# Cross-entropy with label smoothing: other transfer widths, and a second row that follows into the first row's buffers

## The chip, the cores and the metric

The kernel runs on one core of one Trainium2 chip. The metric is device time in microseconds (us). Most executions agree within 0.3%. Kernels are compared only within the same rounds.

## The reference

For 256 rows of 32000 float32 logits, with one label each and smoothing 0.1:

```
log_probs = logits - max(logits); log_probs -= log(sum(exp(log_probs)))
targets   = 0.1/32000 everywhere, + 0.9 at the label
out       = -sum(targets * log_probs)        # one number per row
```

What is costly is one sum of exponentials (ScalarE) and one plain sum (VectorE) over 32.77 MB, which must be read once.

## The kernel before

Each of 128 partitions holds two rows, one after the other in memory. A row arrives in tiles of some thousand columns over all partitions. Per tile, VectorE adds the two halves of the tile and accumulates, and ScalarE takes exponentials and accumulates; what they write besides the sums is scratch that nobody reads (`jd`, `ja`, `jt`). The second row's tiles get narrower, so that little is left to do after the last byte.

```python
WIDTHS = (
    (8000, 8000, 8000, 8000),
    (8000, 6272, 4736, 3648, 2688, 2048, 1536, 1216, 1024, 832),
)
RING_MIN = 4736
TURN_MAX = 3648
...
    ring = ctx.enter_context(tc.tile_pool(name="ring", bufs=3))
    tail = ctx.enter_context(tc.tile_pool(name="tail", bufs=1))
    junk = ctx.enter_context(tc.tile_pool(name="junk", bufs=1))
    turn = ctx.enter_context(tc.tile_pool(name="turn", bufs=3))
...
    def load(w: int, col: int, name: str):
        if w >= RING_MIN:
            xt = ring.tile([P, max(WIDTHS[0])], FP32, name="xt", tag="xt")
        else:
            xt = tail.tile([P, w], FP32, name=name, tag=name)
        ...   # the very first tile in two halves, on the SyncE and ScalarE queues
            nc.sync.dma_start(out=xt[:, :w], in_=x[:, col : col + w])
...
    def sum_exps(xt, w: int, out: bass.AP) -> None:
        if w > TURN_MAX:
            ja = junk.tile([P, max(WIDTHS[0])], BF16, name="ja", tag="ja")   # one buffer
        else:
            ja = turn.tile([P, TURN_MAX], BF16, name="jt", tag="jt")         # three in turn
        nc.scalar.activation(out=ja[:, :w], in_=xt[:, :w], func=AF.Exp, accum_out=out)
```

After the last tile: the logarithm (Ln) of the last row's sum on ScalarE, two transposes on TensorE, two small operations on VectorE, and one transfer of 1 KB out.

The softmax here doesn't subtract the row's maximum and nothing guards it: scores larger than these inputs give would overflow.

## Time and profile before

| | before |
|---|---|
| time, median of 6 runs | 84.85 us (84.72 to 84.95) |
| span in the profile | 83.2 us |
| last tile | 832 columns, exponential from 79.24 us, Ln from 80.20 us |
| busy: ScalarE, VectorE | 58.8 us, 37.1 us |

The span runs from the first to the last instruction; the time is some 1.8 us longer. Read the profile from its end. ScalarE and VectorE wait for the same transfer for each tile. VectorE is the faster one, so it is nearly always waiting when a tile lands: its starts are a clock for the stream. The lines are in the prediction.

### The profile page before, as it was taken

To read this page: it belongs to the slowest core of one execution; us is meant where nothing else is said; L and a number is where in the kernel's file an instruction comes from. 1 tells how busy PE (TensorE), PEld (TensorE's weight loads), DVE (VectorE), ACT (ScalarE), POOL (GpSimd) and SP (SyncE) were. 2 spreads that over 40 slices of the span, in tenths; PEclk is the share of its full clock that TensorE was granted. 3 is DMA by queue.
4 is the path that set the end of the run, shared out by engine and by line. 5 is a ranking of instruction groups with operands and counts; after the bars stand their busy time and mean duration, and the time that the engine had idled before them with its cause. 6 is when DMAs were issued, how large, how long until landed. Compare 5 with 4: busy or idle time off the path is not lost.

```text
span 83.2 us, 230 instructions
## 1 busy us (share of the span) xinstructions
PE 7.0 (8%) x23; PEld 5.0 (6%) x23; DVE 37.1 (45%) x35; ACT 58.8 (71%) x31; POOL 5.7 (7%) x19
## 2 busy tenths in 40 slices
PE   0000000000000000000000010000000000899020
PEld 0000000000000000000000000000000000787000
DVE  0000005950495009910397017922944736754860
ACT  5000005997499809994399908997999999999960
POOL 3201640031000000000000040000000000000000
PEclk9999999999999999999999999999999999999995
DMA  5999999997999899989998998998999999999600
GB/s 131 416 416 408 454 423 462 477 447 323 477 493 431 369 431 493 446 369 416 493 462 354 416 439 386 495 447 370 428 420 414 442 407 415 412 414 412 256 0 0
DMA packets 2258, 32.77 MB, mean 394 GB/s; under 512 B 337, under 2 KB 338, under 8 KB 850
## 3 DMA queue, kind: packets, MB, share of 16 engines
q1 hardware_dynamic: 2018, 30.72, 87.4%
q10 hardware_dynamic: 144, 2.05, 5.8%
q0 software_dynamic: 96, 0.00, 0.1%
HBM read 32.77 MB, written 0.00 MB: 394 GB/s over the span
## 4 chain that ended last, share of the span: by engine, by line
DMA 64%; ACT 32%; issue 1%; SPq 0%; PE 0%; DVE 0%; ACTq 0%
DMA xt<-in_logits_dram 40%; DMA xl<-in_logits_dram 23%; ACT ja L188 17%; ACT jt L188 15%; SPq L167 0%; PE lse_t L193 0%; DVE res L284 0%; ACT lse L279 0%; ACTq L188 0%
## 5 line engine op out<-in xcount | busy, mean ns | idle before, releaser
L188 ACT ACTIVATE ja<-xt 128x8000 bf16<-128x8000 f32 (+2 forms) x7 | 43.9, 6276 | 20.1 <-DMA xt<-in_logits_dram 20.0
L173 DVE SCALAR_TENSOR_TENSOR jd<-xt 128x4000 f32<-128x4000 f32 (+2 forms) x7 | 27.7, 3954 | 33.6 <-DMA xt<-in_logits_dram 33.6
L188 ACT ACTIVATE jt<-xl 128x3648 bf16<-128x3648 f32 (+6 forms) x7 | 12.2, 1748 | 0.1
L173 DVE SCALAR_TENSOR_TENSOR jd<-xl 128x1824 f32<-128x1824 f32 (+6 forms) x7 | 7.9, 1125 | 5.2 <-DMA xl<-in_logits_dram 5.0
L270 PE MATMUL warm<-xl,ident 128*128 128x256 f32 x20 | 6.1, 471 | 21.4 <-DMA xl<-in_logits_dram 21.4
L270 PEld LDWEIGHTS warm<-xl,ident 128*128 128x128 f32 x20 | 4.8, 246 | 22.5 <-DMA xl<-in_logits_dram 21.7
L193 PE MATMUL loss_t<-ident,loss 128*1 128x128 f32 x1 | 0.4, 372 | 49.2 <-POOL loss L224 49.2
L193 PEld LDWEIGHTS loss_t<-ident,loss 128*1 128x1 f32 x1 | 0.1, 79 | 49.2 <-POOL loss L224 49.2
L226 DVE COPY res<-loss_t 1x128 f32<-1x128 f32 x1 | 0.3, 278 | 4.5 <-PE loss_t L193 4.5
L211 POOL TENSOR_TENSOR half<-sums 128x4 f32<-128x4 f32 x1 | 0.2, 198 | 28.2 <-ACT ja L188 28.2
L125 POOL DMA_INDIRECT gat<-in_logits_dram,flat_idx x2 | 2.0, 1004 | 0.7 <-POOL ident masks.py:199 0.4
L92 ACT ACT_TABLE_LOAD x1 | 1.3, 1283 | 0.9 <-PEq L311 0.9
L188 ACT ACTIVATION_READ_ACCUMULATOR ja<-xt 128x1 f32 x7 | 1.3, 186 | 0.0
L188 ACT ACTIVATION_READ_ACCUMULATOR jt<-xl 128x1 f32 x7 | 1.3, 181 | 0.0
L146 POOL TENSOR_SCALAR weighted<-gat 128x1 f32<-128x1 f32 x1 | 0.8, 763 | 5.8 <-DMA gat<-in_logits_dram,flat_idx 5.8
L105 POOL DMA_DIRECT2D lab<-in_labels_dram x1 | 0.8, 766 | 1.0 <-POOLq L311 1.0
L216 ACT ACTIVATE lse<-half 128x1 f32<-128x1 f32 x1 | 0.2, 203 | 0.6 <-POOL half L211 0.6
L173 DVE DVE_READ_ACCUMULATOR jd<-xt 128x1 f32 x7 | 0.6, 82 | 0.0
L173 DVE DVE_READ_ACCUMULATOR jd<-xl 128x1 f32 x7 | 0.6, 82 | 0.0
L117 POOL TENSOR_TENSOR flat_idx<-rowoff,lab 128x2 int32<-128x2 int32 x1 | 0.2, 197 | 5.4 <-DMA lab<-in_labels_dram 5.4
L193 PE MATMUL lin_t<-ident,done 128*1 128x128 f32 x1 | 0.3, 270 | 3.0 <-DVE done L263 3.0
L282 DVE COPY lin_row<-lin_t 1x128 f32<-1x128 f32 x1 | 0.3, 278 | 0.4 <-PE lin_t L193 0.4
(20 smaller groups left out, 3.8 us busy)
## 6 DMA issues: line engine op xcount, KB each, us to landing
xt<-in_logits_dram SPq DMA_DIRECT2D x4, 4000.0 KB, 21.1
xt<-in_logits_dram SPq DMA_DIRECT2D x1, 3136.0 KB, 19.4
xt<-in_logits_dram SPq DMA_DIRECT2D x1, 2368.0 KB
xt<-in_logits_dram SPq DMA_DIRECT2D x1, 2000.0 KB, 11.5
xt<-in_logits_dram ACTq DMA_DIRECT2D x1, 2000.0 KB, 13.2
xl<-in_logits_dram SPq DMA_DIRECT2D x1, 1824.0 KB, 19.5
xl<-in_logits_dram SPq DMA_DIRECT2D x1, 1344.0 KB, 22.3
xl<-in_logits_dram SPq DMA_DIRECT2D x1, 1024.0 KB, 24.3
```

Of the source, the lines that this page charges most:

```text
L92: nc.scalar.add_instruction(mybir.InstLoadActFuncSet(name=nc.get_next_instruction_name(), act_func_set_id=tbl, ins=[], outs=[],))
L105: nc.gpsimd.dma_start(out=lab[:], in_=labels.bitcast(I32).rearrange("(p f) -> p f", p=P))
L117: nc.gpsimd.tensor_tensor(out=flat_idx[:], in0=rowoff[:], in1=lab[:].rearrange("p (r two) -> p r two", two=2)[:, :, 0:1], op=ALU.add,)
L125: nc.gpsimd.indirect_dma_start(out=gat[:, r : r + 1], out_offset=None, in_=logits[:], in_offset=bass.IndirectOffsetOnAxis(ap=flat_idx[:, r ...
L146: nc.gpsimd.tensor_scalar(out=weighted[r], in0=gat[:, r : r + 1], scalar1=label_weight, scalar2=None, op0=ALU.mult,)
L173: return nc.vector.scalar_tensor_tensor(out=jd[:, :h], in0=xt[:, :h], scalar=1.0, in1=xt[:, h:w], op0=ALU.mult, op1=ALU.add, accum_out=out,)
L188: nc.scalar.activation(out=ja[:, :w], in_=xt[:, :w], func=AF.Exp, accum_out=out)
L193: nc.tensor.transpose(out=row[:], in_=column, identity=ident[:])
L211: nc.gpsimd.tensor_tensor(out=half[:], in0=sums[:, :, :n], in1=sums[:, :, n:], op=ALU.add)
L226: nc.vector.tensor_copy(out=res[:, :, r : r + 1], in_=loss_t[:])
L270: nc.tensor.matmul(warm[:], lhsT=ident[:], rhs=xt[:, i * WARM_COLS : (i + 1) * WARM_COLS], start=True, stop=True,)
L282: nc.vector.tensor_copy(out=lin_row[:], in_=lin_t[:])
```

## The change

Its intent: a smaller last tile (640 columns instead of 832), and fewer, larger transfers in the first row, whose buffers the second row then fills in pieces.

```diff
 WIDTHS = (
-    (8000, 8000, 8000, 8000),
-    (8000, 6272, 4736, 3648, 2688, 2048, 1536, 1216, 1024, 832),
+    (8000, 12000, 12000),
+    (8576, 6272, 4608, 3456, 2496, 1856, 1408, 1088, 896, 704, 640),
 )
-RING_MIN = 4736
-TURN_MAX = 3648
-WARM_LEFT, WARM_COLS = 5, 256
+FOLLOW = (1, 2, 7)
+TURN_MAX = 3456
+WARM_LEFT, WARM_COLS = 6, 256
...
-    ring = ctx.enter_context(tc.tile_pool(name="ring", bufs=3))
+    wide = ctx.enter_context(tc.tile_pool(name="wide", bufs=1))
...
+    for r in range(R):
+        for b in range(len(FOLLOW)):
+            t = sum(FOLLOW[:b])
+            parts = (WIDTHS[0][b : b + 1], WIDTHS[1][t : t + FOLLOW[b]])
+            widths = parts[r]
+            w = max(sum(parts[0]), sum(parts[1]))
+            buf = wide.tile([P, w], FP32, name=f"wide{b}_{r}", tag=f"wide{b}")
+            ...   # buffers: slices of buf, one after the other
+    ...           # what is left over (640 columns) in a buffer of its own
...
+        with tc.issue_after(exps.ins):      # first row's Ln behind the 8576-column exponential
+            nc.scalar.activation(out=lse[:], in_=total[:, 1, :], func=AF.Ln)
```

More of the change, by code (lines that the diff above doesn't have):

```diff
@@ L154, with load @@
     res = small.tile([1, P, R], FP32, name="res", tag="res")
-    def load(w: int, col: int, name: str):
-        if w >= RING_MIN:
-            xt = ring.tile([P, max(WIDTHS[0])], FP32, name="xt", tag="xt")
-        else:
-            xt = tail.tile([P, w], FP32, name=name, tag=name)
+    assert R == 2 and len(FOLLOW) == len(WIDTHS[0])
+    buffers = []
+    for r in range(R):
[5 more added lines that the diff above has]
+            buf = wide.tile([P, w], FP32, name=f"wide{b}_{r}", tag=f"wide{b}")
+            at = 0
+            for v in widths:
+                buffers.append(buf[:, at : at + v])
+                at += v
+    for t in range(sum(FOLLOW), len(WIDTHS[1])):
+        w = WIDTHS[1][t]
+        buffers.append(tail.tile([P, w], FP32, name=f"tail{t}", tag=f"tail{t}")[:])
+    def load(w: int, col: int):
+        xt = buffers.pop(0)
         if col == 0:
@@ L166, in load @@
         else:
-            nc.sync.dma_start(out=xt[:, :w], in_=x[:, col : col + w])
+            nc.sync.dma_start(out=xt, in_=x[:, col : col + w])
         return xt
@@ L181, in sum_logits, with sum_exps @@
         )
-    def sum_exps(xt, w: int, out: bass.AP) -> None:
+    def sum_exps(xt, w: int, out: bass.AP):
         if w > TURN_MAX:
@@ L187, in sum_exps @@
             ja = turn.tile([P, TURN_MAX], BF16, name="jt", tag="jt")
-        nc.scalar.activation(out=ja[:, :w], in_=xt[:, :w], func=AF.Exp, accum_out=out)
+        return nc.scalar.activation(
+            out=ja[:, :w], in_=xt[:, :w], func=AF.Exp, accum_out=out
+        )
     def row_of(column: bass.AP, name: str):
@@ L194, in row_of, with finish_first_row @@
         return row
+    assert R == 2
     col = 0
-    for r in range(R - 1):
-        n = len(WIDTHS[r])
-        sums = small.tile([P, 2, n], FP32, name=f"sums{r}", tag=f"sums{r}")
-        for t, w in enumerate(WIDTHS[r]):
-            xt = load(w, col, f"xl{r}_{t}")
-            col += w
-            sum_logits(xt, w, sums[:, 0, t : t + 1])
-            sum_exps(xt, w, sums[:, 1, t : t + 1])
-        while n > 1:
-            assert n % 2 == 0
-            n //= 2
-            half = small.tile([P, 2, n], FP32, name=f"half{r}_{n}", tag=f"half{r}_{n}")
+    n = len(WIDTHS[0])
+    sums = small.tile([P, 2, n], FP32, name="sums", tag="sums")
+    for t, w in enumerate(WIDTHS[0]):
+        xt = load(w, col)
+        col += w
+        sum_logits(xt, w, sums[:, 0, t : t + 1])
+        sum_exps(xt, w, sums[:, 1, t : t + 1])
+    def finish_first_row(part, exps) -> None:
+        total = sums[:, :, 0:1]
+        for t in range(1, n):
+            acc = small.tile([P, 2, 1], FP32, name=f"acc{t}", tag=f"acc{t}")
             nc.gpsimd.tensor_tensor(
-                out=half[:], in0=sums[:, :, :n], in1=sums[:, :, n:], op=ALU.add
+                out=acc[:], in0=total, in1=sums[:, :, t : t + 1], op=ALU.add
             )
-            sums = half
-        lse = small.tile([P, 1], FP32, name=f"lse{r}", tag=f"lse{r}")
-        nc.scalar.activation(out=lse[:], in_=sums[:, 1, :], func=AF.Ln)
-        lin = small.tile([P, 1], FP32, name=f"lin{r}", tag=f"lin{r}")
-        nc.gpsimd.tensor_tensor(out=lin[:], in0=sums[:, 0, :], in1=weighted[r], op=ALU.add)
-        scaled = small.tile([P, 1], FP32, name=f"scaled{r}", tag=f"scaled{r}")
+            total = acc[:]
+        lin = small.tile([P, 1], FP32, name="lin0", tag="lin0")
+        nc.gpsimd.tensor_tensor(
+            out=lin[:], in0=total[:, 0, :], in1=weighted[0], op=ALU.add
+        )
+        scaled = small.tile([P, 1], FP32, name="scaled0", tag="scaled0")
         nc.gpsimd.tensor_scalar(
@@ L222 @@
         )
-        loss = small.tile([P, 1], FP32, name=f"loss{r}", tag=f"loss{r}")
+        lse = small.tile([P, 1], FP32, name="lse0", tag="lse0")
+        with tc.issue_after(exps.ins):
+            nc.scalar.activation(out=lse[:], in_=total[:, 1, :], func=AF.Ln)
+        loss = small.tile([P, 1], FP32, name="loss0", tag="loss0")
         nc.gpsimd.tensor_tensor(out=loss[:], in0=scaled[:], in1=lse[:], op=ALU.add)
-        loss_t = row_of(loss[:], f"loss_t{r}")
-        nc.vector.tensor_copy(out=res[:, :, r : r + 1], in_=loss_t[:])
+        loss_t = row_of(loss[:], "loss_t0")
+        with tc.issue_after(part.ins):
+            nc.vector.tensor_copy(out=res[:, :, 0:1], in_=loss_t[:])
     r = R - 1
-    n = len(WIDTHS[r])
+    last = len(WIDTHS[r]) - 1
     elast = psum.tile([P, 1], FP32, name="elast", tag="elast")
@@ L240 @@
     for t, w in enumerate(WIDTHS[r]):
-        left = n - 1 - t
-        xt = load(w, col, f"xl{r}_{t}")
+        left = last - t
+        xt = load(w, col)
         col += w
@@ L247 @@
         if left == 0:
-            sum_exps(xt, w, elast[:])
+            exps = sum_exps(xt, w, elast[:])
         elif left <= 2:
-            sum_exps(xt, w, pairs[2 - left][:, 1:2])
+            exps = sum_exps(xt, w, pairs[2 - left][:, 1:2])
         else:
-            sum_exps(xt, w, esum[:, t : t + 1])
+            exps = sum_exps(xt, w, esum[:, t : t + 1])
+        if t == 0:
+            finish_first_row(part, exps)
         if left == 2:
```

## The prediction

> **What bounds the kernel now.** I read, in order, the busy shares, the slices, the chain that ended last, and then the ScalarE and VectorE instructions in order of time. First the page:
>
> ```profile
> PE 7.0 (8%) x23; PEld 5.0 (6%) x23; DVE 37.1 (45%) x35; ACT 58.8 (71%) x31; POOL 5.7 (7%) x19
> ...
> ACT  5000005997499809994399908997999999999960
> ...
> DMA  5999999997999899989998998998999999999600
> ```
>
> No engine is busy throughout, but the DMA row is: from the second slice to the 37th there is no hole. The kernel is one stream of 32.77 MB, and ScalarE's exponentials run beside it; ScalarE is also full from about two thirds on. The question is which of the two sets the end there. The chain:
>
> ```profile
> DMA 64%; ACT 32%; issue 1%; SPq 0%; PE 0%; DVE 0%; ACTq 0%
> ...
> 48.17 19.52 DMA xl<-in_logits_dram
> 67.69 0.02 issue
> 67.72 7.63 ACT jt L188 x5
> ```
>
> It goes back from the end over ScalarE to 67.7 us and over transfers before that, so it looks as if the last 12 us were ScalarE's. The starts of its instructions say something finer (columns: start, duration, engine, line, operation):
>
> ```profile
> 50.31 6.87 ACT L188 ACTIVATE ja<-xt 128x8000 bf16<-128x8000 f32 x1 [1.75 <-DMA xt<-in_logits_dram]
> 57.08 0.19 ACT L188 ACTIVATION_READ_ACCUMULATOR ja<-xt 128x1 f32 x1
> 57.77 5.43 ACT L188 ACTIVATE ja<-xt 128x6272 bf16<-128x6272 f32 x1 [0.50 <-DMA xt<-in_logits_dram]
> 63.10 0.19 ACT L188 ACTIVATION_READ_ACCUMULATOR ja<-xt 128x1 f32 x1
> 63.41 4.15 ACT L188 ACTIVATE ja<-xt 128x4736 bf16<-128x4736 f32 x1
> 67.47 0.19 ACT L188 ACTIVATION_READ_ACCUMULATOR ja<-xt 128x1 f32 x1
> 67.72 3.24 ACT L188 ACTIVATE jt<-xl 128x3648 bf16<-128x3648 f32 x1
> ...
> 78.18 1.06 ACT L188 ACTIVATE jt<-xl 128x1024 bf16<-128x1024 f32 x1
> 79.14 0.19 ACT L188 ACTIVATION_READ_ACCUMULATOR jt<-xl 128x1 f32 x1
> 79.24 0.88 ACT L188 ACTIVATE jt<-xl 128x832 bf16<-128x832 f32 x1
> 80.02 0.15 ACT L188 ACTIVATION_READ_ACCUMULATOR jt<-xl 128x1 f32 x1
> 80.20 0.26 ACT L279 ACTIVATE lse<-elast,done 128x1 f32<-128x1 f32 x1
> ```
>
> VectorE, which is faster, shows the arrivals: it starts the 2688, 2048, 1536 and 1216 columns at 71.03, 73.52, 75.40 and 76.91 us, each time after 0.5 to 1.2 us of idleness ended by the transfer, and ScalarE starts the same columns at 70.96, 73.44, 75.39 and 76.90. So ScalarE is at no tile more than about 0.05 us late: the widths balance it against the stream, and the stream sets the pace to the end. After the last arrival (about 79.2) comes the exponential of 832 columns, then some 3 us of fixed tail.
>
> **Two rates from these lines.** Arrival: the 8000-column tiles start 9.49, 9.47 and 9.51 us apart (21.84, 31.33, 40.80, 50.31), the 1024-column one 1.28 after its forerunner. The line through 9.49 and 1.28 is t(w) = 0.075 us + 1.177 ns x w. It gives 7.46, 5.65, 3.24 and 2.49 for 6272, 4736, 2688 and 2048 columns; the starts show 7.46, 5.64, 3.24, 2.48. A column is 512 bytes over 128 partitions, so this is 435 GB/s, plus 0.075 us per transfer. ScalarE: durations of 6.87 (8000) and 1.06 (1024) give 0.833 ns per column + 0.206 us. In the small scratch the next one may start at once (78.18 + 1.06 = 79.24, exactly the next start), so its pitch is 0.833w + 0.206. In the wide scratch the build has each exponential wait for the one before it, so the accumulator read counts in full: 57.08 + 0.19 is 6.96 after 50.31, plus about 0.03 for the signal, so 0.833w + 0.33.
>
> **What the Trainium skill says.**
> - "DMA: Bandwidth & Descriptors", section "Where 436 GB/s comes from": 435.2 GB/s is the ceiling of the 16 ports. The trace agrees: 435 GB/s in the fit, so the stream has nothing left to gain per byte.
> - "ScalarE: Activation LUTs", section "What ACT_TABLE_LOAD costs": an ACTIVATE takes 186 ns + 0.833 ns per element, and neighbours overlap by about 93 ns. The slope agrees, the intercept is 206 ns here; I use the trace's.
> - "SBUF — State Buffer", section "Who interferes with whom": DMA contends with no compute engine. The trace agrees as far as it goes: with ScalarE busy throughout from 63.4 to 67.7 us the stretch moved 434 GB/s.
> - "DMA: Bandwidth & Descriptors", section "How a descriptor splits into AXI transactions": a read that does not start on a 256-byte boundary costs a partial transaction. All column offsets of before are multiples of 64 columns (256 bytes); no run here shows an unaligned one yet.
>
> **The change part by part.**
> 1. *First row in 3 transfers instead of 4, second in 11 instead of 10.* 14 tiles before, 14 after, the same bytes. One 0.075 us per transfer is removed and one added: the last byte should arrive when it did, at 79.24.
> 2. *Buffers.* Before, each load from the fourth on waited for a buffer of the ring. Now the two 12000s wait for nothing; 8576 waits for ScalarE to leave the first tile (about 20.4), 6272 and 4608 for it to leave the second (about 36.9), the rest for the third (about 51.1). At those times the stream still has work until 40.75, 50.92 and 63.88 us by the fit. The last three also wait for landed transfers (8576, 6272, 4608), all over long before. So no wait on the path goes, and none comes: the queue was already full.
> 3. *First row's Ln* moves behind the 8576-column exponential, where ScalarE is busy. Its 0.20 us lies mostly inside that tile's accumulator read and signal; I charge 0.04.
> 4. *Last tile* 640 instead of 832: 192 x 0.833 ns = 0.16 us less between last arrival and Ln. This is the gain intended.
> 5. *Widths against ScalarE.* By the fit the second tile (20000 columns) arrives at 21.84 + 4000 x 1.177 ns = 26.55. Arrivals and ScalarE starts from there, start = later of arrival and the previous start plus its pitch:
>
> 12000: 26.55, 26.55; 12000: 40.75, 40.75; 8576: 50.92, 51.08 (10.33 of pitch against 10.17 of transfer); 6272: 58.38, 58.59; 4608: 63.88, 64.15; 3456: 68.02, 68.19; 2496: 71.03, 71.28; 1856: 73.29, 73.56; 1408: 75.02, 75.31; 1088: 76.38, 76.69; 896: 77.51, 77.80; 704: 78.41, 78.75; 640: 79.24, 79.54.
>
> ScalarE is busy without a gap from the second 12000 on and reaches the last tile 0.30 us late; before it was at most 0.04 late there. From that start to Ln took 0.96 for 832 columns (79.24 to 80.20), so 0.80 for 640: Ln at 80.34 against 80.20. Sum: +0.30 of lateness - 0.16 of shorter tile = +0.14 us. VectorE's last sums (640 columns cost about 0.60, the addition 0.16) end near 80.1, before that. TensorE warms up on 2496 columns that arrive when the 2688 did, nine pairs instead of ten: no change of the tail. The span goes from 83.2 to about 83.3, the time from 84.89 to about 85.0.
>
> **Rivals.**
> - *ScalarE does not fall behind* (the wide-scratch wait costs less than 0.13, or the Ln nothing). Then only the shorter last tile counts: -0.1 to -0.16, about 84.75. For it: the wide pitch is never seen back to back in the trace, since a transfer ended each wait. Against it: even with the small pitch everywhere, 0.206, 8576 and 12000 leave no slack, and the tail widths lose some hundredths each.
> - *The stream gets faster*: larger packets (48,000 bytes a row instead of 32,000) or fewer pauses on waits. Against it: 435 GB/s is already the fit and the DMA row has no holes; all of the per-transfer cost of the first row is 4 x 0.075 = 0.3 us. It would make 84.5 at best.
> - *The stream gets slower.* 12000 columns are 187.5 x 256 bytes, so the third tile starts half a unit off in memory, and what lies in the third wide buffer may be off on the write side. If only the first piece of a row pays, it is a few hundredths; if every piece did, 5% of the 24,000 columns concerned would be 1.4 us, about 86.4. The profile of before holds no such transfer, so I can only call it unlikely.
> - *A buffer wait starves the queue*: the large buffers are freed late and all at once. The margins of part 2 are 3.9, 13.8 and 12.8 us, so I hold it for excluded.
>
> **Range and chances.** The terms that I trust are -0.16 and +0.30, each uncertain by 0.15; the end of the stream by 0.2. The three runs of before differ by 0.17. So 85.0, with 84.6 to 85.4 for 8 in 10. A gain of 2% would need 1.7 us, which the stream does not have: 1%. A loss of 2% needs the third rival at its worst: 2%.
>
> **What would show it.** In the changed profile, ScalarE's starts should show no idle time ended by a transfer after the second 12000; the 8576 should start at the previous accumulator read's end, not at an arrival; VectorE should be released by transfers 0.2 to 0.3 us before ScalarE on the late tiles; the last exponential should start at about 79.5 and Ln at 80.3. I am wrong if VectorE's releases come at other times than the list above (the stream changed), or if ScalarE again starts with VectorE (no lateness: the first rival).

## The result, and the profile after

The changed kernel takes 84.84 us (median of 6 runs, 84.74 to 84.90), before 84.85: ratio 1.000, interval 0.9987 to 1.0013. The span is 83.0 us. The page of the changed kernel:

```profile
PE 6.7 (8%) x21; PEld 4.8 (6%) x21; DVE 36.9 (44%) x35; ACT 58.1 (70%) x31; POOL 10.2 (12%) x19
...
ACT  5000002999102999970499999999999999999960
...
DMA  6999998999888999888998979999999999999500
...
DMA 47%; ACT 45%; issue 3%; SPq 0%; PE 0%; DVE 0%; ACTq 0%
```

The totals have hardly moved, but the chain has: ScalarE's share of it rose from 32% to 45%. In its row of slices ScalarE is full from the 21st on. Its starts, in order of time (start, duration, engine, line, operation; in brackets idle time before, and what ended it):

```profile
40.63 10.20 ACT L203 ACTIVATE ja<-wide 128x12000 bf16<-128x12000 f32 x1 [3.88 <-DMA wide<-in_logits_dram]
50.74 0.19 ACT L203 ACTIVATION_READ_ACCUMULATOR ja<-wide 128x1 f32 x1
50.95 7.35 ACT L203 ACTIVATE ja<-wide 128x8576 bf16<-128x8576 f32 x1
58.21 0.19 ACT L203 ACTIVATION_READ_ACCUMULATOR ja<-wide 128x1 f32 x1
58.30 0.19 ACT L244 ACTIVATE lse<-acc 128x1 f32<-128x1 f32 x1
58.43 5.43 ACT L203 ACTIVATE ja<-wide 128x6272 bf16<-128x6272 f32 x1
...
63.98 4.04 ACT L203 ACTIVATE ja<-wide 128x4608 bf16<-128x4608 f32 x1
...
77.54 0.93 ACT L203 ACTIVATE jt<-wide 128x896 bf16<-128x896 f32 x1
...
79.25 0.72 ACT L203 ACTIVATE jt<-tail 128x640 bf16<-128x640 f32 x1
79.87 0.15 ACT L203 ACTIVATION_READ_ACCUMULATOR jt<-tail 128x1 f32 x1
80.05 0.26 ACT L304 ACTIVATE lse<-elast,done 128x1 f32<-128x1 f32 x1
```

After 40.63 us no bracket names a transfer: from the second 12000 on, nothing in ScalarE's starts depends on the stream. VectorE, as the clock of arrivals, first before, then after:

```profile
73.52 1.23 DVE L173 SCALAR_TENSOR_TENSOR jd<-xl 128x1024 f32<-128x1024 f32 x1 [0.92 <-DMA xl<-in_logits_dram]
...
75.40 0.96 DVE L173 SCALAR_TENSOR_TENSOR jd<-xl 128x768 f32<-128x768 f32 x1 [0.65 <-DMA xl<-in_logits_dram]
...
76.91 0.79 DVE L173 SCALAR_TENSOR_TENSOR jd<-xl 128x608 f32<-128x608 f32 x1 [0.55 <-DMA xl<-in_logits_dram]
```

```profile
73.00 1.13 DVE L188 SCALAR_TENSOR_TENSOR jd<-wide 128x928 f32<-128x928 f32 x1 [0.74 <-DMA wide<-in_logits_dram]
...
74.68 0.89 DVE L188 SCALAR_TENSOR_TENSOR jd<-wide 128x704 f32<-128x704 f32 x1 [0.54 <-DMA wide<-in_logits_dram]
...
75.98 0.73 DVE L188 SCALAR_TENSOR_TENSOR jd<-wide 128x544 f32<-128x544 f32 x1 [0.40 <-DMA wide<-in_logits_dram]
...
77.05 0.63 DVE L188 SCALAR_TENSOR_TENSOR jd<-wide 128x448 f32<-128x448 f32 x1 [0.34 <-DMA wide<-in_logits_dram]
```

Two things are to be seen. ScalarE starts the 896 columns (VectorE's 448 pairs) at 77.54 where VectorE starts them at 77.05: it is 0.49 us late. And the stream itself has become faster at its end. VectorE's starts lie 1.30 and 1.07 us apart for 1088 and 896 columns; the fit of before (0.075 us + 1.177 ns per column) gives 1.36 and 1.13. That was not predicted.

To see it in the stream, take from the trace each packet's duration (a packet is one partition's piece of one tile) and subtract its bytes over 27.2 GB/s, one sixteenth of the 435.2 GB/s that the prediction cites as the ceiling. This is called the excess below. The median of what is left, in ns, by tile of the second row:

```
before:   8000  6272  4736  3648  2688  2048  1536  1216  1024   832
          11.0  12.6  12.5  12.5  12.7  11.8  12.1  12.2  10.4  11.6
changed:  8576  6272  4608  3456  2496  1856  1408  1088   896   704   640
           7.8  10.6  10.4   7.8   7.9   8.1   7.9   8.0   8.2   8.5   7.9
```

A tile has 128 packets, 8 for each of the 16 engines if they share evenly, so by estimate 4 ns per packet are 0.03 us per tile, and a third of a microsecond over eleven tiles. The build gives a candidate. The buffers of before all begin 128 bytes beside a multiple of 256 in their partition. In the changed kernel the third wide buffer, which takes the tiles from 3456 to 704, falls on a multiple of 256 by accident, because a 12000-column buffer is 187.5 x 256 bytes long. The candidate does not fit every tile: the 8576 and the 640 columns are written 128 bytes off and show 7.8 and 7.9 ns too (the 8576 with a mean of 10.8).

### The profile page after: what moved, and what is told of

Read it like the earlier page. It is cut to its first block, busy times and chain, and to the rows that moved or that the text cites. A ratio compares the mean times of both kernels' runs of the same rounds, so it can differ in the third digit from the quotient of the medians.

```text
span 83.0 us, 226 instructions
## 1 busy us (share of the span) xinstructions
PE 6.7 (8%) x21; PEld 4.8 (6%) x21; DVE 36.9 (44%) x35; ACT 58.1 (70%) x31; POOL 10.2 (12%) x19
## 4 chain that ended last, share of the span: by engine, by line
DMA 47%; ACT 45%; issue 3%; SPq 0%; PE 0%; DVE 0%; ACTq 0%
DMA wide<-in_logits_dram 47%; ACT ja L203 33%; ACT jt L203 11%; SPq L182 0%; PE lse_t L210 0%; DVE res L309 0%; ACT lse L304 0%; ACT lse L244 0%; ACTq L203 0%
## 5 line engine op out<-in xcount | busy, mean ns | idle before, releaser
L203 ACT ACTIVATE ja<-wide 128x12000 bf16<-128x12000 f32 (+4 forms) x6 | 44.1, 7350 | 21.2 <-DMA wide<-in_logits_dram 21.2
L188 DVE SCALAR_TENSOR_TENSOR jd<-wide 128x6000 f32<-128x6000 f32 (+11 forms) x13 | 35.0, 2695 | 39.0 <-DMA wide<-in_logits_dram 39.0
L203 ACT ACTIVATE jt<-wide 128x3456 bf16<-128x3456 f32 (+6 forms) x7 | 11.2, 1603 | 0.0
L295 PE MATMUL warm<-wide,ident 128*128 128x256 f32 x18 | 5.8, 492 | 11.5 <-DMA wide<-in_logits_dram 11.5
L230 POOL TENSOR_TENSOR acc<-acc,sums 128x2 f32<-128x2 f32 x1 | 4.4, 4427 | 14.0 <-ACT ja L203 14.0
L295 PEld LDWEIGHTS warm<-wide,ident 128*128 128x128 f32 x18 | 4.5, 258 | 12.6 <-DMA wide<-in_logits_dram 11.8
L203 ACT ACTIVATION_READ_ACCUMULATOR jt<-wide 128x1 f32 x7 | 1.3, 186 | 0.0
L203 ACT ACTIVATION_READ_ACCUMULATOR ja<-wide 128x1 f32 x6 | 1.1, 186 | 0.0
L188 DVE DVE_READ_ACCUMULATOR jd<-wide 128x1 f32 x13 | 1.1, 82 | 0.0
L203 ACT ACTIVATE jt<-tail 128x640 bf16<-128x640 f32 x1 | 0.7, 719 | 0.0
## 6 DMA issues: line engine op xcount, KB each, us to landing
wide<-in_logits_dram ACTq DMA_DIRECT2D x1, 2000.0 KB, 13.8
```

What stands on the lines that cost most here:

```text
L188: return nc.vector.scalar_tensor_tensor(out=jd[:, :h], in0=xt[:, :h], scalar=1.0, in1=xt[:, h:w], op0=ALU.mult, op1=ALU.add, accum_out=out,)
L203: return nc.scalar.activation(out=ja[:, :w], in_=xt[:, :w], func=AF.Exp, accum_out=out)
L230: nc.gpsimd.tensor_tensor(out=acc[:], in0=total, in1=sums[:, :, t : t + 1], op=ALU.add)
L295: nc.tensor.matmul(warm[:], lhsT=ident[:], rhs=xt[:, i * WARM_COLS : (i + 1) * WARM_COLS], start=True, stop=True,)
```

## The experiments

Two questions: is ScalarE's lateness what takes the gain back (rival: the stream still sets the end), and why is the stream's end faster (where the bytes are written, against the queue's state or chance)?

### Writes moved by 128 bytes

```diff
+    shift = ctx.enter_context(tc.tile_pool(name="shift", bufs=1))
+    pad = shift.tile([nc.NUM_PARTITIONS, 32], FP32, name="pad", tag="pad")
+    nc.gpsimd.memset(pad[:], 0.0)
     ring = ctx.enter_context(...)      # or: wide = ...
```

In the kernel before, this brings all loads to multiples of 256 bytes (the scratch moves along):

> The kernel before with a 128-byte pad ahead of its buffers, so that every load is written to a multiple of 256 bytes in a partition instead of 128 bytes beside one. Theory A (write alignment costs packets of the stream about 4 ns each): the median packet excess over size / 27.2 GB/s falls from about 12 to about 8 ns in the second row, the stream ends about 0.3 us earlier, ScalarE can still keep up, and the time falls by 0.2 to 0.35 us, to about 84.55. Rival B (the faster end of the stream in the changed kernel comes from the queue's state or from chance, not from where the bytes go): packets and time stay, 84.85 +- 0.1.

Measured: 84.35 us against 84.78 for the kernel before, ratio 0.9942 (0.9922 to 0.9962). Median packet excess 7.8 to 8.7 ns in every tile; the last packet ends at 78.21 us instead of 78.66. VectorE's starts on 1536 and 1216 columns were 1.88 and 1.51 us after their forerunners; here they are 1.80 and 1.47:

```profile
73.04 1.23 DVE L176 SCALAR_TENSOR_TENSOR jd<-xl 128x1024 f32<-128x1024 f32 x1 [0.87 <-DMA xl<-in_logits_dram]
...
74.84 0.96 DVE L176 SCALAR_TENSOR_TENSOR jd<-xl 128x768 f32<-128x768 f32 x1 [0.57 <-DMA xl<-in_logits_dram]
...
76.31 0.79 DVE L176 SCALAR_TENSOR_TENSOR jd<-xl 128x608 f32<-128x608 f32 x1 [0.51 <-DMA xl<-in_logits_dram]
```

A pad of 128 bytes, and nothing else, is worth more than the whole change. It was run again:

> The shifted kernel before once more, beside the version with slack on the same chip: 84.35 +- 0.1, ratio to before about 0.994. If writes to multiples of 256 bytes are what counts, every tile from the second on shows about 8.5 ns per packet over size / 27.2 GB/s again.

Measured: 84.31 against 84.80, ratio 0.9935 (0.9921 to 0.9948), median excess 7.8 to 8.7 ns in every tile. And the kernel before was traced again, unchanged:

> The kernel before, unchanged, for a second trace of it. If where the bytes are written sets the packets' time, the median excess over size / 27.2 GB/s is again 11 to 13 ns in the second row and the last arrival again about 0.3 us after that of the changed kernel; if the state of the queue or chance sets it, the excess may come out at 8 to 9 ns in some tiles.

Measured: 84.83 us; median excess 10.4 to 12.7 ns in every tile from the third on, last packet at 78.56 us. Its Ln starts at 80.09 us and its span is 83.0, so this trace is closer to before's median than the first.

The packets are not all of it. In the second row VectorE starts 0.46 to 0.57 us after a tile's last packet in both traces of the kernel before, and 0.35 to 0.47 us in both of the shifted one. So an engine that waits is also released about 0.1 us sooner; the traces don't show by what.

In the changed kernel the same pad brings the first two wide buffers to multiples of 256 and puts the third off:

> The changed kernel with the same 128-byte pad: its first two wide buffers and the tail come to multiples of 256 bytes, and the third wide buffer, with the last seven loads but one, goes off by 128. Theory A: the seven small loads take about 12 ns more than size / 27.2 GB/s per packet instead of 8, the 8576, 6272 and 4608 ones about 8; the stream ends about 0.15 us later than in the changed kernel, but ScalarE is 0.3 to 0.5 us late there, so the time stays within 0.1 us of 84.84. Rival B: the packets show the pattern of the unshifted kernel. Rival C (ScalarE isn't late, the stream sets the end): the time rises with the stream, by 0.15 us.

Measured: 84.74 us against 84.78, ratio 0.9993 (0.9972 to 1.0013); the time stays, as expected from a late ScalarE. The packets followed only in part. In the third buffer, now off by 128, the median excess is 7.8 and 7.9 ns at first (3456, 2496 columns) and rises to 10.5 (704); the means go from 8.0 to 11.8. The expected 12 throughout did not come. So a write off the multiple may cost, and need not: here, as with the 640 columns of the changed kernel, tiles that follow aligned ones cost nothing at first.

With the wide buffers rounded up too (`w = -(-max(...) // 64) * 64`), everything is aligned:

> The changed kernel with the 128-byte pad and its wide buffers rounded up to whole 256 bytes, so that every load is written to a multiple of 256 bytes. All packets about 8 ns over size / 27.2 GB/s; the stream ends at about 78.2 us. Theory (in the changed kernel ScalarE is late from the second 12000 on, and a faster stream can give only what the third tile's earlier arrival gives): the time falls by no more than 0.1 us more than with the shift alone, to 84.65 to 84.8, while the same alignment gave the kernel before 0.43 us; ScalarE is 0.4 to 0.6 us late at the last tiles. Rival C (the stream sets the end here too): it falls by 0.3 us or more, to 84.5 or less.

Measured: 84.79 against 84.90, ratio 0.9984 (0.9964 to 1.0004). The last packet ends at 78.21 us, as in the shifted kernel before, but Ln starts later. First the shifted kernel before, then this one:

```profile
79.64 0.26 ACT L282 ACTIVATE lse<-elast,done 128x1 f32<-128x1 f32 x1
```

```profile
79.98 0.26 ACT L307 ACTIVATE lse<-elast,done 128x1 f32<-128x1 f32 x1
```

The same alignment is worth 0.58% in one kernel and nothing measurable in the other: rival C, that the stream sets the changed kernel's end, is out.

This pair also answers a rival to the writes: the pad moves the scratch as well. By a build of the kernels, the scratch lies the same relative to multiples of 256 bytes here and in the shifted changed kernel, and of the large buffers only the third differs. Its tiles have a mean excess of 7.8 to 8.5 ns here and 7.9 to 11.8 there. So it is where the loads are written that counts, and not the scratch.

### ScalarE out of the way

```diff
-            out=ja[:, :w], in_=xt[:, :w], func=AF.Exp, accum_out=out
+            out=ja[:, : w // 2], in_=xt[:, : w // 2], func=AF.Exp, accum_out=out
```

The results are wrong (relative error 0.0635 in both); loads and VectorE's work are unchanged.

> The kernel before with each exponential over the first half of its tile only (wrong results on purpose), so that ScalarE is never late and the stream alone sets the end. Theory: ScalarE was hardly late, so little is won: VectorE's last addition, which ends at 79.99 us in the trace of before, takes over, Ln at about 80.0 instead of 80.2 and the time falls by 0.1 to 0.2 us, to about 84.65.

> The changed kernel with the same halving (wrong results on purpose). Theory: the shorter last tile and the faster end of the stream are real and only ScalarE's lateness takes them back; with ScalarE out of the way the last addition on VectorE ends at about 79.4 and Ln starts at about 79.5 instead of 80.05: time down by 0.5 us, to about 84.3, that is 0.3 to 0.4 below the halved kernel before. Rival (the change gains nothing at the stream's end): within 0.1 us of the halved kernel before.

Measured, before at 84.80: the halved kernel before takes 84.76 (ratio 0.9989, 0.9975 to 1.0003), the halved changed kernel 84.22 (0.9927, 0.9913 to 0.9942). ScalarE's last tile and Ln, halved before and halved changed:

```profile
79.10 0.55 ACT L188 ACTIVATE jt<-xl 128x416 bf16<-128x416 f32 x1 [0.30 <-DMA xl<-in_logits_dram]
...
80.00 0.26 ACT L281 ACTIVATE lse<-elast,done 128x1 f32<-128x1 f32 x1 [0.29 <-DVE done L265]
```

```profile
78.64 0.47 ACT L203 ACTIVATE jt<-tail 128x320 bf16<-128x320 f32 x1 [0.20 <-DMA tail<-in_logits_dram]
...
79.44 0.26 ACT L304 ACTIVATE lse<-elast,done 128x1 f32<-128x1 f32 x1 [0.27 <-DVE done L288]
```

Now both are released by transfers to the end, and VectorE's last addition releases Ln. The changed stream, with its smaller last tile, would have let the kernel end 0.54 us sooner than the kernel before. The expectation for before (0.1 to 0.2 us won) was too high by about 0.1; the contrast is as expected, somewhat larger.

### A part of the lateness taken away

```diff
-TURN_MAX = 3456
+TURN_MAX = 6272
-    turn = ctx.enter_context(tc.tile_pool(name="turn", bufs=3))
+    turn = ctx.enter_context(tc.tile_pool(name="turn", bufs=2))
```

> The changed kernel with the exponentials of 6272 and 4608 columns in the rotating scratch (two buffers of 6272), so that neither waits for its forerunner's accumulator. Theory (ScalarE is late from the second 12000 on): its pitch falls by 0.12 to 0.14 us at the 6272-column tile and little at the 8576 one, where the Ln of the first row now shows its own 0.1 us; all starts after it come that much earlier: time down by 0.1 to 0.2 us, about 84.7. Rival C (the stream sets the end): no change, 84.84 +- 0.05.

Measured: 84.61 us against 84.78, ratio 0.9974 (0.9956 to 0.9991). The 4608 columns follow the 6272 at 63.76 - 58.35 = 5.41 us here and at 63.98 - 58.43 = 5.55 us in the changed kernel: 0.14 us, as expected.

```profile
58.35 5.41 ACT L203 ACTIVATE jt<-wide 128x6272 bf16<-128x6272 f32 x1
...
63.76 4.03 ACT L203 ACTIVATE jt<-wide 128x4608 bf16<-128x4608 f32 x1
```

Ln starts at 79.83 instead of 80.05. Of these 0.22 us, 0.14 are this tile's and 0.04 the 8576's; the rest was there already at the second 12000, which landed 0.05 us sooner in this trace. The changed kernel itself did not run in this call; its shifted form did, at 84.74.

### The first row in four 8000s

```diff
-    (8000, 12000, 12000),
+    (8000, 8000, 8000, 8000),
-FOLLOW = (1, 2, 7)
+FOLLOW = (1, 1, 2, 5)
```

(With the scratch sized by the widest tile of both rows.)

> The changed kernel's second row and its arrangement of buffers, but the first row in four 8000s. ScalarE has slack before the 8576 columns, so they start on arrival (about 50.8 us) and not 0.15 us later; all these loads are written 128 bytes beside a multiple of 256. Theory: the 12000s cost ScalarE 0.15 us of lateness, which is won here, but by theory A the stream is slow again and arrivals then bind: Ln within 0.1 us of the changed kernel's, time 84.7 to 84.85, and ScalarE starts within 0.1 us of VectorE on late tiles. Rival B (the fast end of the stream belongs to the new second row): stream ends at about 78.3 as in the changed kernel, ScalarE 0.2 to 0.3 us late, time about 84.65.

Measured: 85.15 us against 84.78, ratio 1.005 (1.0024 to 1.0075): slower, which neither theory expected. What was expected inside is there: 8576 columns start on arrival at 50.88 us, all tiles from the third on have a median excess of 10 to 13 ns, as theory A has it for buffers 128 bytes off, the last packet ends at 78.64 us, ScalarE starts within 0.1 us of VectorE on late tiles, and Ln starts at 80.00 us. But the span ends at 83.2. This kernel has 16 loads instead of 15. Eight semaphores serve the transfers in turn, so the output gets another one, and at the end SyncE checks them in a fixed order. In the changed kernel the output's is the sixth check, in this one the second, and SyncE waits in it for 0.72 us, with four checks of about 0.06 us still to come. A changed kernel with one idle load more:

```diff
+    extra = small.tile([P, 32], FP32, name="extra", tag="extra")
...
+            nc.sync.dma_start(out=extra[:], in_=x[:, :32])
```

> The changed kernel with one more load, of 32 columns into a buffer that nobody reads, so that there are 16 loads as in the kernel with four 8000s. The output transfer then has the second semaphore in the list that SyncE goes through at the end and not the sixth. Theory: SyncE waits for the output first and makes four of the other checks after it: the span grows by about 0.2 us and the time by 0.2 to 0.4, to about 85.15, with the tiles' starts moved by less than 0.1. Rival: the four 8000s lost their 0.3 us in the stream or in ScalarE; then this kernel stays within 0.1 us of 84.84.

Measured: 85.11 us against 84.90, ratio 1.0017 (0.9998 to 1.0036); against the changed kernel aligned, it is 0.3 us longer. SyncE's own waits in the changed kernel and in this one (what waited, for what, us in total, times, longest):

```profile
SPq L350 <- DMA out_dram<-res: 0.5, 1, 0.5
```

```profile
SPq L352 <- DMA out_dram<-res: 0.7, 1, 0.7
```

The wait for the output begins 0.2 us earlier relative to the issue of the output, and so is 0.2 us longer; the checks come after it. That settles about 0.2 us of the four 8000s' loss, with blemishes: in this trace all starts also lie 0.1 us later than in the changed kernel's, and the last transpose took 0.37 us instead of 0.27. Another 0.2 us of the loss lies outside the span (time minus span is 1.94 to 2.10 us in the six runs of the four 8000s, about 1.8 in those of all other kernels), and stays unexplained.

### Two versions meant to beat both

Aligned buffers, scratch in turn from 6144 columns down, and widths by the measured rates so that ScalarE keeps up:

> A version meant to beat both: aligned writes, first row 9984, 11008, 11008, second row 8384, 6080, 4608, 3392, 2496, 1920, 1472, 1152, 960, 832, 704, scratch in turn from 6144 columns down with two buffers. By the measured rates (0.044 us + 1.1763 ns per column for a transfer; 0.833 ns per column + 0.19 us for ScalarE, + 0.33 where it waits for its forerunner) ScalarE is at most 0.1 us late anywhere and under 0.05 at the end; Ln at about 79.55 us, time about 84.25, 0.1 less than the shifted kernel before. If lateness was not what took the gain back, it is no faster than the changed kernel with aligned writes.

Measured: 84.48 against 84.90, ratio 0.9937 (0.9917 to 0.9957), with Ln at 79.80. ScalarE is 0.1 us late at most, but Ln comes 0.25 us later than worked out. The first tile, in two halves on two queues and larger here, was taken for the cause. Back to 8000 there (diff against the changed kernel; the pad, the rounding and the scratch are as in the first try):

```diff
-    (8000, 12000, 12000),
-    (8576, 6272, 4608, 3456, 2496, 1856, 1408, 1088, 896, 704, 640),
+    (8000, 12416, 11584),
+    (8384, 6080, 4608, 3392, 2496, 1920, 1472, 1152, 960, 832, 704),
-FOLLOW = (1, 2, 7)
+FOLLOW = (1, 2, 6)
```

> The version with slack again, but with a first tile of 8000 columns, then 12416 and 11584: in the first try the larger first tile delayed everything by about 0.3 us[...]. Last arrival 0.25 us earlier than there, Ln at about 79.6 us, time about 84.25, level with or 0.1 below the shifted kernel before of the same call.

Measured: 84.32 against 84.80, ratio 0.9934 (0.9920 to 0.9947), Ln at 79.61; level with the shifted kernel before (84.31). Both beat the kernel before by 0.65%. The simpler one is the kernel before with a 128-byte pad.

The two tries do not differ beyond noise (0.9937 and 0.9934), and their traces don't bear out the supposed cause. Up to 7 us the first try had moved as much as the others. Between 7 and 8 us it moved at 363 GB/s, where all other traces have 427 to 430; that cost about 0.17 us, and the distance stayed. What stalled it is not known. The slow packets of every first tile are something else: most start before the second queue's first packet.

## Why the prediction was right or wrong

The time was right: 85.0 predicted, within 84.6 to 85.4, measured 84.84. So was the main mechanism: ScalarE falls behind and takes back what the smaller last tile gives. A loss of 0.14 us was forecast, hardly more than the runs spread, and none was found. Two terms of the sum were mis-sized in opposite directions: the stream's end came sooner than forecast, and ScalarE was later against it. They belong together, since where ScalarE sets the end, a tile that lands sooner only waits longer for it. So the close number does not confirm the terms one by one; that they offset each other as well as this is luck.

- *ScalarE late from the second 12000 on* (part 5): shown. No transfer ends a wait after 40.63 us; taking 0.18 us of its waits away moves the end by about as much; taking it out wins 0.6 us; a faster stream wins nothing.
- *The list of starts*: right in shape, high by 0.13 us at 8576 columns and by 0.29 at 640. The second 12000 came 0.12 us sooner, Ln of the first row cost about 0.01 where 0.04 was charged (6272 start 7.48 us after 8576, of which 7.47 are the tile and its wait), and the pitch in the rotating scratch is about 0.19 us + 0.833 ns per column, not 0.206, over seven tiles. The 0.206 was read from exponentials that had waited for their tile; the prediction's own line for 832 columns (0.88 us) gives 0.187.
- *The last byte arrives when it did* (part 1): wrong, and this is the step that failed. 14 tiles before and after do make no difference, but a tile's fixed cost isn't one number: it depends on where it is written. The last packet ended 0.23 us sooner, and the release after it came 0.11 us sooner as well. The rival "the stream gets faster" was dismissed because the fit already gave 435 GB/s; the fit's 0.075 us per transfer held the gain. With everything aligned the starts give about 0.044. So ScalarE's lateness before the last tile was larger than the 0.30 us of the prediction: 79.25 against an arrival at about 78.75 (78.64 in the halved kernel, whose last packet ended 0.11 us earlier), 0.5 us.
- *Last tile, -0.16 us* (part 4): right. From the last exponential's start to Ln it is 0.96 us before (second trace: 79.13 to 80.09) and 0.80 after (79.25 to 80.05). VectorE's sum of 640 columns took 0.49 us, not 0.60, which changes nothing.
- *The sum by the traces*, changed against the second trace of before: last packet 78.33 against 78.56, -0.23; from there to the last exponential's start 0.92 against 0.57, +0.35; from there to Ln -0.16. Together -0.04 us, with spans of 83.0 in both. Predicted were 0, +0.30 and -0.16. The halved kernels, where nothing is late, split the middle term: there ScalarE's last exponential starts 0.53 us after the last packet before the change and 0.42 after it. So the arrival moved by about -0.35 and the lateness by about +0.47.
- *The rival of an unaligned read* (12000 columns end half a unit off): did not show. The third tile, the only one read from an offset of 128 bytes, has 8.3 ns of median excess. The prediction's 5% for the worst case rests on no number of the record. The guess added there, that the write side might matter, pointed to the right place with the wrong sign: the change moved the third buffer on to the multiple, not off it.
- *Buffer waits*: excluded rightly; the slices of the transfers show no hole. Two of its three margins do not follow from part 2's times, which give 20.4, 14.0 and 12.8 us instead of 3.9, 13.8 and 12.8; all are wide.

## What to carry to other kernels

When a stream and an engine are balanced to a few hundredths, a gain at the one is worth only what the other leaves: first find out, by halving the engine's work, what the stream alone would give. A fixed cost that a straight-line fit shows is not yet a constant; look at the packets. And a buffer's address is a parameter: rounding it to 256 bytes costs a pad, and won 0.6% in the kernel whose end hung on the stream, nothing measurable in the other.

## What the Trainium skill lacked or had wrong

- "DMA: Bandwidth & Descriptors", section "How a descriptor splits into AXI transactions", speaks of where a read starts. No page that I read speaks of the write side: with all loads written to multiples of 256 bytes a packet took 8 to 9 ns more than its bytes at 27.2 GB/s, with all of them 128 bytes off mostly 10 to 13, which is 0.58% and 0.65% of the kernel's time in two calls. The waiting engine was also released about 0.1 us sooner after the last packet. Off the multiple it does not always cost (7.8 ns in some tiles); what decides it, and by what mechanism, is open.
- The same page, section "Issuing engines are not separate DMA queues", has transfers of two queues interleave on the same engines. The traces agree: with two queues at work, from 4 to 7 us, the stream moved 424 to 431 GB/s, against 432 to 434 with one, from 20 to 40 us. The slow packets of the first tile (70 to 95 ns above their bytes on average in its SyncE half, 10 to 15 in the other) mostly start before the second queue's first packet, which comes at about 2.8 us. So nothing is lacking or wrong here.
- "SBUF — State Buffer", section "Who interferes with whom", says that a VectorE instruction with two SBUF inputs contends with a GpSimd instruction that reads SBUF. The trace agrees, so nothing is lacking here: in the changed kernel a GpSimd addition of 128x2 elements beside VectorE's 8576-column sum took 4.43 us and ended with that sum, where its neighbour took 0.19. It lies off the path. In the changed kernel:

```profile
L230 POOL TENSOR_TENSOR acc<-acc,sums 128x2 f32<-128x2 f32 x1 | 4.4, 4427 | 14.0 <-ACT ja L203 14.0
L230 POOL TENSOR_TENSOR acc<-sums 128x2 f32<-128x2 f32 x1 | 0.2, 192 | 15.6 <-ACT ja L203 15.6
```

- No page that I read has what the number of transfers costs at the end: with the output's semaphore second instead of sixth among SyncE's last checks, about 0.2 us of span.
- "ScalarE: Activation LUTs", section "What ACT_TABLE_LOAD costs", gives 186 ns + 0.833 ns per element and an overlap of about 93 ns. The prediction set 206 ns against it, but the page is right: in the changed kernel's rotating scratch the exponentials took 186 to 189 ns + 0.833 ns per column, and followed one another at about the same distance. Those that had waited for a transfer or for their forerunner's scratch took 204 to 207 ns + 0.833 ns per column; the section has no figure for these.
